# First rows scaled in place and transposed in a written order, one bank and the stores moved, and the first MLP product's weights copied ahead of the splits

## The chip, the cores and the metric

The kernel runs on one core of a Trainium2 chip. The metric is the device time of one execution in microseconds, as the median of several runs. Before the change it is 2446.93 us (three runs, 2443.65 to 2447.63).

## What is computed

One layer of a decoder trunk on a sequence of 512 rows of 2048 channels, all in float32. Cut to what matters:

```
h = rmsnorm(x, g_mix)
cb, cc, cv, q, k, v, f_logit, gate_c, gate_a = split(h @ w_in)
conv_branch = (cb * causal_dwconv(cc * cv, conv_w)) @ w_conv_out
attn_branch = forgetting_attention(q, k, v, log_sigmoid(f_logit + b_f)) @ w_attn_out
x = x + (sigmoid(gate_c + b) * conv_branch + sigmoid(gate_a + b) * attn_branch) @ w_mix_out
h = rmsnorm(x, g_mlp)
x = x + square(relu(h @ w_ff1)) @ w_ff2
out = rmsnorm(x, g_final)
```

Here rmsnorm(x, g) is x / sqrt(mean(x*x) + eps) * g, row by row. Nearly all the time goes to the large products: w_in (2048 x 10248), w_ff1 (2048 x 8192) and w_ff2 (8192 x 2048).

## The kernel before

**Products.** A product in float32 is made of three: each operand is split into a high part (ACT's copy to the rounded type fp32r, buffer th for weights) and a low part (DVE's difference between the operand and its high part, buffer tl). PE then adds high x high, high x low and low x high into a bank of PSUM (lines 149, 151, 153 with weights standing and rows moving; lines 167, 169, 172 the other way round). There are two buffers th and two tl.

**Groups.** The products with w_in and w_ff1 are made in groups of two by two blocks by a scheme that needs seven products in place of eight (A11, A12, S4, S3, S2, A22, S1; class Group). The rows' operands of the same names (A11, A12, A22 and the sums S1 to S4) are made once and held in tiles. A group has four accumulators a, b, c, d, and its argument `banks` says in which of the eight banks each lies. `begin` makes A11 (into a) and A12 (into b), `rest` the other five. A product is one step of a pipeline (class Pipe, line 188 on): in each step the sources of one product are split on ACT and DVE, the product split a step before is put on PE, and the one before that is evacuated from its bank (`snap`, ACT, line 294; `plus`, DVE, line 112). Other work hangs on the steps by `pipe.fill(n, work)`, which runs it n steps later. Within `with manual():` the order of the instructions on each engine is the order in which the program writes them; outside, the framework's scheduler orders them by priority and readiness.

**The opening (lines 554 to 627).** The rows x come in four blocks t of 128 rows (tile xn, line 562), each of 1 MB, all queued on SP ahead of the first weights (line 274). For each block ACT squares and sums the rows (line 496), DVE adds the sums up (line 491) and POOL takes the inverse root (line 492), which gives a factor r per row. DVE puts r on the diagonal of a 128 x 128 tile dg (line 526). PE multiplies 128 x 128 pieces of the rows with dg (line 530), four to a bank, banks 6 and 7 in turn: that transposes and scales at once. Each such float32 matmul appears twice in the trace, as two passes. DVE multiplies the bank with the gain per channel (tile cols) into h, in two instructions, one for even and one for odd pieces of channels (line 535). Then the halves of A11, A12 and A22 that this block of rows fills are split (lines 105 and 106). All of this is ordered by the scheduler, together with what follows: five groups of which only `begin` is made at first, gV0 (a part of the attention's V) and four key-and-query groups (`heads`), while the sums for S1 to S4 are made beside them. Among these groups b lies in bank 3 for all five.

**The MLP's start (lines 1530 to 1552).** The last rows of the second norm are turned and summed while the first group g0 of w_ff1 runs its A11 and A12, in a written order: `Q2.sums(3, behind)` makes the high parts of S1, S3, S2, S4 on ACT (line 1152) and the low parts of S4 and S3 on DVE, then `g0.rest` begins with S4, whose weights ACT copies to th (line 248). `behind` holds the low parts of S2 and S1.

**The MLP's groups.** There are 16. Each evacuated half j is squared into r and summed (`sums`), and one step later split into rh and r and stored by two transfers on POOL's queue (`store`, lines 1248 to 1252). r and rh have one buffer each. Accumulator a lies in bank 4 for the first group and in banks 4 and 2 in turn from the second on.

## Time and profile before

| | us |
|---|---|
| median of three runs | 2446.93 (2443.65 to 2447.63) |
| the profiled execution | 2438.63 |
| its span, first to last instruction | 2436.9 |
| PE busy | 2412.2 |
| DVE busy | 1969.9 |
| ACT busy | 1169.0 |
| POOL busy | 238.5 |

PE is the matmul engine and PEld its weight loads, which run beside it; DVE is the vector engine, ACT the scalar engine, POOL GpSimd, SP SyncE, which issues loads. L149 is line 149 of the kernel. A row of the timeline gives start and length in us, the engine, the line, the operation, what is written and read, the shape, a count, and in brackets the idle time ahead of it with what ended it. A row of waits gives who waited for whom, the total in us, how often, and the longest. A row of stretches gives the stretch, its length, then busy time and count of PE, PEld, DVE, ACT and POOL, the granted clock as a share of full, the share of DMA and GB/s. A row of groups gives the line, the operation, its tiles and shape, the count, busy time in us and mean ns of one, and the idle time ahead.

### The profile page before, as it was taken

To read this page: it belongs to the slowest core of one execution; us is meant where nothing else is said; L and a number is where in the kernel's file an instruction comes from. 1 tells how busy PE (TensorE), PEld (TensorE's weight loads), DVE (VectorE), ACT (ScalarE), POOL (GpSimd) and SP (SyncE) were. 2 spreads that over 40 slices of the span, in tenths; PEclk is the share of its full clock that TensorE was granted. 3 is DMA by queue.
4 is the path that set the end of the run, shared out by engine and by line. 5 is a ranking of instruction groups with operands and counts; after the bars stand their busy time and mean duration, and the time that the engine had idled before them with its cause. 6 is when DMAs were issued, how large, how long until landed. Compare 5 with 4: busy or idle time off the path is not lost. (4 is left out here: it accounts for less than half of the span.)

```text
span 2436.9 us, 39812 instructions
## 1 busy us (share of the span) xinstructions
PE 2412.2 (99%) x17199; PEld 2242.7 (92%) x17199; DVE 1969.9 (81%) x1633; ACT 1169.0 (48%) x1184; POOL 238.5 (10%) x383
## 2 busy tenths in 40 slices
PE   8999999999999999999999999999999999999998
PEld 8999999999999998888899999999998888888886
DVE  7877677768887786735789888988988888888888
ACT  6443444444445563235556666665655333333334
POOL 0100011111210210100000000000010001100000
PEclk9999999999999999999999999999999999999999
DMA  7654434445664655536555655656588577655662
GB/s 251 182 180 156 152 122 147 153 142 163 210 197 131 204 169 169 186 121 216 164 199 179 211 205 185 242 187 219 190 292 284 199 244 242 232 186 198 230 225 87
DMA packets 268707, 466.17 MB, mean 191 GB/s; under 512 B 10524, under 2 KB 176532, under 8 KB 268404
## 3 DMA queue, kind: packets, MB, share of 16 engines
q1 hardware_dynamic: 224768, 283.72, 36.9%
q0 software_dynamic: 42896, 178.28, 20.0%
q8 instruction: 135, 2.21, 0.4%
q10 hardware_dynamic: 868, 1.62, 0.2%
q14 instruction: 40, 0.33, 0.0%
HBM read 369.74 MB, written 93.85 MB: 190 GB/s over the span
## 5 line engine op out<-in xcount | busy, mean ns | idle before, releaser
L248 ACT ACTIVATE th<-x 128x2048 fp32r<-128x2048 f32 (+2 forms) x280 | 513.2, 1833 | 499.1 <-PE a L151 150.1
L109 DVE TENSOR_TENSOR tl<-x,th 128x2048 fp32r<-128x2048 f32 (+2 forms) x280 | 610.6, 2181 | 144.2 <-ACT th L248 142.9
L109 DVE TENSOR_TENSOR x<-x,x 128x2048 f32<-128x2048 f32 (+1 forms) x108 | 246.9, 2287 | 36.8 <-DMA x<-in_w_ff_dram 36.7
L248 ACT ACTIVATE th<-y 128x2048 fp32r<-128x2048 f32 x66 | 126.7, 1922 | 200.8 <-PE a L169 99.1
L149 PE MATMUL a<-ST,th 128*128 128x256 f32 x768 | 177.6, 277 | 0.9 <-ACT o L294 0.9
L151 PE MATMUL a<-ST,th 128*128 128x256 f32 x768 | 177.3, 277 | 0.0
L167 PE MATMUL a<-th,us 128*128 128x512 f32 x512 | 161.1, 392 | 1.7 <-ACT x L1382 0.8
L248 ACT ACTIVATE th<-t 128x2048 fp32r<-128x2048 f32 x46 | 88.2, 1918 | 152.8 <-PE a L169 87.2
L109 DVE TENSOR_TENSOR tl<-y,th 128x2048 fp32r<-128x2048 f32 x66 | 150.8, 2286 | 10.8 <-ACT th L248 10.6
L169 PE MATMUL a<-th,us 128*128 128x512 f32 x512 | 158.5, 389 | 0.0
L106 DVE TENSOR_TENSOR tl<-raw,th 128x2048 fp32r<-128x2048 f32 x32 | 73.4, 2292 | 94.9 <-ACT th L105 94.7
L149 PEld LDWEIGHTS a<-ST,th 128*128 128x128 f32 x768 | 144.3, 188 | 1.3 <-ACT o L294 1.3
L109 DVE TENSOR_TENSOR tl<-t,th 128x2048 fp32r<-128x2048 f32 x46 | 105.3, 2289 | 48.7 <-ACT th L248 48.7
L151 PEld LDWEIGHTS a<-ST,th 128*128 128x128 f32 x768 | 144.3, 188 | 0.0
L482 PE MATMUL pn<-th,m 128*128 128x512 f32 x512 | 134.4, 391 | 0.0
L149 PE MATMUL a<-S,th 128*128 128x256 f32 x576 | 133.8, 278 | 0.0
L151 PE MATMUL a<-S,th 128*128 128x256 f32 x576 | 132.8, 276 | 0.0
L172 PE MATMUL a<-tl,us 128*128 128x512 f32 x512 | 126.6, 389 | 0.0
L167 PEld LDWEIGHTS a<-th,us 128*128 128x128 f32 x512 | 96.0, 188 | 26.2 <-DVE x L1384 3.4
L149 PE MATMUL d<-ST,th 128*128 128x256 f32 x512 | 118.4, 277 | 0.0
L151 PE MATMUL d<-ST,th 128*128 128x256 f32 x512 | 118.3, 277 | 0.0
L172 PEld LDWEIGHTS a<-tl,us 128*128 128x128 f32 x512 | 96.1, 188 | 19.9
(341 smaller groups left out, 6236.7 us busy)
## 6 DMA issues: line engine op xcount, KB each, us to landing
x<-in_w_in_dram SPq DMA_DIRECT2D x86, 1024.0 KB, 5.8
x<-in_w_ff_dram SPq DMA_DIRECT2D x64, 1024.0 KB, 7.8
y<-in_w_ff_dram SPq DMA_DIRECT2D x64, 1024.0 KB, 7.0
us<-s_d POOLq DMA_DIRECT2D x42, 1024.0 KB, 8.9
s_d<-rh POOLq DMA_DIRECT2D x32, 896.0 KB, 6.6
s_d<-r POOLq DMA_DIRECT2D x32, 896.0 KB, 7.6
raw<-in_w_mix_out_dram SPq DMA_DIRECT2D x24, 1024.0 KB, 5.1
g_d<-o POOLq DMA_DIRECT2D x32, 256.0 KB, 2.6
```

The lines of the kernel that those rows point to most:

```text
L106: nc.vector.tensor_tensor(out=lo, in0=src, in1=hi.bitcast(F32), op=ALU.subtract)
L109: nc.vector.tensor_tensor(out=out, in0=a, in1=b, op=ALU.subtract)
L149: nc.tensor.matmul(o, hi[:, q, js], Sh, start=first and q == 0 and j == 0, stop=False, skip_group_check=True)
L151: nc.tensor.matmul(o, hi[:, q, js], Sl, start=False, stop=False, skip_group_check=True)
L167: nc.tensor.matmul(o, Sh[:, ts], hi[:, q, :], start=begin, stop=False, skip_group_check=True)
L169: nc.tensor.matmul(o, Sl[:, ts], hi[:, q, :], start=False, stop=False, skip_group_check=True)
L172: nc.tensor.matmul(o, Sh[:, ts], lo[:, q, :], start=False, stop=q == nq - 1, skip_group_check=True)
L248: nc.scalar.activation(out=self.hi, in_=self.src, func=AF.Copy)
L482: nc.tensor.matmul(ps[t], A[t][e], w[:, q, :], start=first, stop=last)
```

## The change

It has five parts.

1. *The opening.* `block` is replaced by `scaled` (the rows are multiplied with r in place, on DVE, in two or four pieces), `turn` (16 transposes with the identity into four banks at once) and `gained` (one instruction per bank, even and odd pieces together). H is renumbered so that both lie in one tile. Block 0 and block 1 are done in a written order (`rows_in`); blocks 2 and 3 are left to the scheduler.
2. *Loads.* The first two weight loads of gV0 are queued on SP between the rows of block 1 and those of block 2.
3. *Banks.* The second key-and-query group's b lies in bank 6. In the MLP, a alternates the other way: bank 2 for the second group, then 4, and so on; the last group's c changes with it.
4. *Stores.* In all MLP groups but the last two, the store of the second half comes one step later.
5. *The MLP's start.* The copy of S4's weights to th is made right behind A22's split, ahead of the four sums' high parts.

On PE, at the program's start; ptr is the bank into which rows are turned, dg the diagonal and ident the identity, th and A the weights and rows of the first products a and b. Before:

```order
L573 MATMUL pv<-ident,rows 128x88
L530 MATMUL ptr<-dg,xn 128x128 x36
L167 MATMUL a<-th,A_146 128x256
L530 MATMUL ptr<-dg,xn 128x128 x4
L167 MATMUL a<-th,A_146 128x256
L530 MATMUL ptr<-dg,xn 128x128 x4
L169 MATMUL a<-th,A_146 128x256 x2
```

And now, where the line numbers are those of the changed kernel:

```order
L590 MATMUL pv<-ident,rows 128x88
L535 MATMUL ptr<-ident,xn 128x128 x32
L167 MATMUL a<-th,A_142 128x256 x2
L169 MATMUL a<-th,A_142 128x256
L167 MATMUL b<-th,A_143 128x256 x2
L169 MATMUL a<-th,A_142 128x256
L167 MATMUL a<-th,A_142 128x256 x2
```

Before, block 2's pieces were turned ahead of and among the first matmuls of a; now blocks 0 and 1 come first, and blocks 2 and 3 follow in two runs of 16 within a's end and b. Two matmuls of b stand ahead of a's fourth.

On DVE, at the same place; v is the sum of squares, r the factor, h the rows turned and gained, A_142 and A_146 are A11, and x_147 the first weights. Before:

```order
L491 TENSOR_REDUCE v<-ss_144 128x1
L526 TENSOR_SCALAR dg<-ident,r 128x128
L642 CAST identb<-ident 128x128
L574 COPY cols<-pv 128x88
L491 TENSOR_REDUCE v<-ss_144 128x1
L535 TENSOR_TENSOR h_148<-ptr,cols 128x2x128
L535 TENSOR_TENSOR h_149<-ptr,cols 128x2x128
L526 TENSOR_SCALAR dg<-ident,r 128x128
```

And now:

```order
L491 TENSOR_REDUCE v<-ss_140 128x1
L529 TENSOR_SCALAR xn<-xn,r 128x512
L591 COPY cols<-pv 128x88
L529 TENSOR_SCALAR xn<-xn,r 128x512 x3
L549 TENSOR_TENSOR h_144<-ptr,cols 128x2x2x128 x2
L678 CAST identb<-ident 128x128
L549 TENSOR_TENSOR h_144<-ptr,cols 128x2x2x128
L491 TENSOR_REDUCE v<-ss_140 128x1
L529 TENSOR_SCALAR xn<-xn,r 128x1024 x2
L549 TENSOR_TENSOR h_144<-ptr,cols 128x2x2x128 x5
L106 TENSOR_TENSOR A_142<-h_144,A_142 128x8x128
L109 TENSOR_TENSOR tl<-x_147,th 128x2048
```

Block 1's reduction stood ahead of all gains; three gains of block 0 now stand ahead of it, and the first weights' low part stands between A11's two halves.

On ACT, at the start of the MLP; ST are the rows' operands (the first row is A22's high part, the L1152 and L1189 rows those of S1, S3, S2 and S4), x_12097 and x_12086 the weights of S4, and o the evacuated A11. Before:

```order
L105 ACTIVATE ST<-down 128x512
L1152 ACTIVATE ST<-down 128x512
L1152 ACTIVATE ST<-up 128x512 x2
L1152 ACTIVATE ST<-down 128x512
L248 ACTIVATE th<-x_12097 128x2048
L294 ACTIVATE o<-a 128x512
```

And now:

```order
L105 ACTIVATE ST<-down 128x512
L248 ACTIVATE th<-x_12086 128x2048
L1189 ACTIVATE ST<-down 128x512
L1189 ACTIVATE ST<-up 128x512 x2
L1189 ACTIVATE ST<-down 128x512
L294 ACTIVATE o<-a 128x512
```

The weights' copy has moved ahead of the four high parts; DVE's order is the same there. Beyond these places, only the stores of part 4 (on ACT and DVE) and the order of the sums beside the key-and-query groups differ.

The diff:

```diff
 
 
         def __init__(self, view, c1, c2, w, ST, mm, banks, put, scale=1.0, extra={}, nq=KT // 2, spot=None):
-            self.extra, self.nq, self.spot = extra, nq, spot
+            self.extra, self.nq, self.spot, self.s4 = extra, nq, spot, None
             self.view, self.cs, self.w, self.ST, self.mm, self.banks = view, (c1, c2), w, ST, mm, banks
             self.put, self.scale, self.at, self.X, self.A = put, scale, {}, {}, {}
 
...
                 self.put(1, 1, r["d1"])
                 self.put(0, 1, r["s4"])
 
-            pipe.step(self.product("S4", (1, 1), "c", True), after=next(turns), guest=True)
+            pipe.step(self.s4 or self.product("S4", (1, 1), "c", True), after=next(turns), guest=True)
             hook("S4")
             p = self.product("S3", (0, 1), "d", True)
             p.evict = s3
...
                 self.tiles(n)
             self.h1 = self.quad(pair(PLACE["S1"], F32, "h1"))
             self.h2 = self.quad(ph.tile([P, 2, D], F32, tag="h", name="h2"))
-            self.H = {(0, 0): self.h1[:, 1], (1, 0): self.h1[:, 0], (0, 1): self.h2[:, 1], (1, 1): self.h2[:, 0]}
+            self.H = {(i, par): h[:, par] for i, h in enumerate((self.h1, self.h2)) for par in range(2)}
 
         def moving(self, n):
             return moving(self.ST[n])
...
         def put(self, n, src, ts=slice(0, HS)):
             split(src[:, :, ts], self.ST[n][:, 0, :, ts], self.ST[n][:, 1, :, ts])
 
-        def block(self, xt, part, t):
+        def scaled(self, xt, part, e, n=2):
             r = rstd_of(part)
-            i, ts = t // 2, slice(t % 2 * P, (t % 2 + 1) * P)
-            dg = const.tile([P, P], F32, tag="dg", name="dg", bufs=2)
-            nc.vector.tensor_scalar(out=dg, in0=ident, scalar1=r, scalar2=None, op0=ALU.mult)
-            for c in range(4):
-                pt = bank(6 + c % 2, "ptr")
+            for c in range(n):
+                h = xt[:, c * D // n:(c + 1) * D // n]
+                if e == "A":
+                    nc.scalar.activation(out=h, in_=h, func=AF.Copy, scale=r)
+                else:
+                    nc.vector.tensor_scalar(out=h, in0=h, scalar1=r, scalar2=None, op0=ALU.mult)
+
+        def turn(self, xt, banks):
+            pts = [bank(b, "ptr") for b in banks]
+            for c, pt in enumerate(pts):
                 for k in range(4):
-                    nc.tensor.matmul(pt[:, k * P:(k + 1) * P], xt[:, (4 * c + k) * P:(4 * c + k + 1) * P], dg,
-                                     start=True, stop=True)
-                p2 = pt.rearrange("p (q two b) -> p two q b", two=2, b=P)
-                g2 = self.gT[:, 4 * c:4 * c + 4].rearrange("p (q two) -> p two q", two=2)
-                for par in range(2):
-                    nc.vector.tensor_tensor(out=self.H[i, par][:, 2 * c:2 * c + 2, ts], in0=p2[:, par],
-                                            in1=g2[:, par].unsqueeze(2).to_broadcast([P, 2, P]), op=ALU.mult)
-            if i == 0:
-                self.put("A11", self.H[0, 0], ts)
-                self.put("A12", self.H[0, 1], ts)
-            else:
-                self.put("A22", self.H[1, 1], ts)
+                    nc.tensor.transpose(pt[:, k * P:(k + 1) * P], xt[:, (4 * c + k) * P:(4 * c + k + 1) * P], ident)
+            return pts
+
+        def gained(self, t, pts, cs=range(4), act=False):
+            ts = slice(t % 2 * P, (t % 2 + 1) * P)
+            for c in cs:
+                o = (self.h1, self.h2)[t // 2][:, :, 2 * c:2 * c + 2, ts]
+                if act:
+                    for k in range(4):
+                        nc.scalar.activation(out=o[:, k % 2, k // 2], in_=pts[c][:, k * P:(k + 1) * P], func=AF.Copy,
+                                             scale=self.gT[:, 4 * c + k:4 * c + k + 1])
+                else:
+                    p2 = pts[c].rearrange("p (q two b) -> p two q b", two=2, b=P)
+                    g2 = self.gT[:, 4 * c:4 * c + 4].rearrange("p (q two) -> p two q", two=2)
+                    nc.vector.tensor_tensor(out=o, in0=p2, in1=g2.unsqueeze(3).to_broadcast([P, 2, 2, P]), op=ALU.mult)
+
+        def half(self, n, t):
+            i, par = {"A11": (0, 0), "A12": (0, 1), "A22": (1, 1)}[n]
+            if n not in self.ST:
+                self.tiles(n)
+            self.put(n, self.H[i, par], slice(t % 2 * P, (t % 2 + 1) * P))
 
         def sums(self):
             H = self.H
...
     px = ph.enter_context(phase("px"))
     xin = []
     xp = [pair(2 + i, F32, "xn") for i in range(2)]
-    for t in range(NT):
+    def load_x(t):
         h = xp[t // 2][:, t % 2]
         n = 4 if t == 0 else 2
         for i in range(n):
             nc.sync.dma_start(out=h[:, i * D // n:(i + 1) * D // n], in_=x[t * P:(t + 1) * P, i * D // n:(i + 1) * D // n])
         xin.append(h)
+
+    for t in range(2):
+        load_x(t)
         if t == 0:
             rows = main.tile([NV, P], F32, tag="x3", name="rows")
             r0 = 0
...
         for i in range(4):
             square_part(xin[t][:, i * S:(i + 1) * S], ss1[:, t, i:i + 1], junk[:, i * S:(i + 1) * S])
 
-    for t in (0, 1):
-        squares(t)
-        Q1.block(xin[t], ss1[:, t, :], t)
-    for t in (2, 3):
-        squares(t)
-    Q1.tiles("A22")
-    for t in (2, 3):
-        Q1.block(xin[t], ss1[:, t, :], t)
-
+    def first_loads():
+        for n in "0123":
+            if n in "01":
+                gV0.load(int(n), 0)
+            else:
+                load_x(int(n))
+
+    def rows_in():
+        squares(0)
+        Q1.scaled(xin[0], ss1[:, 0, :], "D", 4)
+        pts = Q1.turn(xin[0], (6, 7, 5, 2))
+        squares(1)
+        Q1.gained(0, pts, range(3))
+        Q1.scaled(xin[1], ss1[:, 1, :], "D")
+        Q1.gained(0, pts, (3,))
+        pts = Q1.turn(xin[1], (0, 1, 6, 7))
+        Q1.gained(1, pts)
+        for n, t in (("A11", 0), ("A11", 1), ("A12", 0), ("A12", 1)):
+            Q1.half(n, t)
 
     def store_v(c0, w):
         def put(i, j, v):
...
     def steady(n):
         return ((2 + n % 2,), (3 - n % 2,), (0,), (1,))
 
-    heads = [gV0] + [kq(hp, ((a,), (3,), (3 + hp % 2 * 3,), (7,))) for hp, a in enumerate((0, 1, 2, 5))]
+    heads = [gV0] + [kq(hp, ((a,), (6 if hp == 1 else 3,), (3 + hp % 2 * 3,), (7,))) for hp, a in enumerate((0, 1, 2, 5))]
+    first_loads()
+    with manual():
+        rows_in()
+    for t in (2, 3):
+        squares(t)
+    for t in (2, 3):
+        Q1.scaled(xin[t], ss1[:, t, :], "DD"[t - 2])
+        Q1.gained(t, Q1.turn(xin[t], (6, 7, 5, 2)))
+        Q1.half("A22", t)
     for g in heads:
         g.begin()
         g.order = ((1, 1), (0, 1), (0, 0), (1, 0))
...
             self.put("A11", c, self.F[0, c][0])
             self.put("A12", c, self.F[0, c][1])
 
-        def sums(self, c, rest=None):
+        def sums(self, c, rest=None, then=lambda: None):
             (a11, a12), (a21, a22) = self.F[0, c], self.F[1, c]
             self.put("A22", c, a22)
+            then()
             add(a22, a21, a22)
             sub(a21, a11, a21)
             sub(a11, a22, a11)
...
                 held.append(c)
             elif j == 0 or ((0, 1) in quarters and (1, 1) in quarters):
                 for n, work in zip(SUMS[j], (sums, store)):
-                    pipe.fill(n + (LATER[j][work is store] if g == DFF // S - 1 else 0), lambda work=work: work(j))
+                    pipe.fill(n + (LATER[j][work is store] if g == DFF // S - 1 else j * (work is store and g < DFF // S - 2)),
+                              lambda work=work: work(j))
 
         return put
 
...
     def banks1(g):
         if g == 0:
             return (4,), (0,), (1,), (7,)
-        return (2 + 2 * (g % 2),), (3,), (1 if g < DFF // S - 1 else 2,), (7 if g < DFF // S - 1 else 5,)
+        return (4 - 2 * (g % 2),), (3,), (1 if g < DFF // S - 1 else 4,), (7 if g < DFF // S - 1 else 5,)
 
     groups = [ff1(g, banks1(g)) for g in range(DFF // S)]
     US = ((4, ("A11", "A12")), (0, ("S2", "S3")), (1, ("S1", "A22")), (2, ("S4",)))
...
         squares_of_rows()
         Q2.gained(1, 3)
         behind = []
-        Q2.sums(3, behind)
+        g0.s4 = g0.product("S4", (1, 1), "c", True)
+        Q2.sums(3, behind, g0.s4.high)
         mean = []
 
         def at(n):
```

## The prediction, made before the changed kernel had run

> **What bounds the kernel now.** I read the page first, then the waits of the matmul engine, then a table of stretches, then the timeline at the places where it waits.
>
> ```profile
> span 2436.9 us, 39812 instructions
> PE 2412.2 (99%) x17199; PEld 2242.7 (92%) x17199; DVE 1969.9 (81%) x1633; ACT 1169.0 (48%) x1184; POOL 238.5 (10%) x383
> ```
>
> PE is busy 2412.2 of 2436.9 us. The change takes one pass away from each of 64 small matmuls and no work from any product, so it can win little beside the 24.7 us in which PE stands. The waits say where that is:
>
> ```profile
> PE pv L573 <- DMA rows<-in_conv_w_dram: 6.1, 1, 6.1
> ...
> PE a L149 <- ACT o L294: 0.9, 2, 0.7
> PE d L142 <- ACT th L248: 0.8, 1, 0.8
> ...
> PE a L153 <- DVE tl L109: 0.6, 1, 0.6
> PE b L149 <- DVE o L112: 0.4, 1, 0.4
> ```
>
> The table (PE, PEld, DVE, ACT and POOL busy with counts, granted clock, DMA share, GB/s) puts them at two places:
>
> ```profile
> 0.00:20.00 20.00, 9.34 (x57) 8.49 (x57) 8.08 (x27) 14.43 (x37) 2.80 (x12) 1.00 0.89 300
> 20.00:40.00 20.00, 19.53 (x168) 19.46 (x169) 17.44 (x29) 10.21 (x8) 0.55 (x1) 1.00 0.79 240
> 40.00:80.00 40.00, 39.59 (x349) 39.43 (x349) 39.11 (x24) 24.05 (x17) 6.39 (x8) 1.00 0.71 211
> 1195.00:1240.00 45.00, 42.73 (x368) 41.98 (x367) 36.38 (x32) 25.01 (x28) 2.32 (x3) 1.00 0.41 129
> 1240.00:1800.00 560.00, 559.79 (x4917) 559.53 (x4916) 492.02 (x365) 350.05 (x350) 32.62 (x60) 1.00 0.59 206
> ```
>
> The opening loses over 10 us, the start of the MLP 2.3, and the MLP's steady groups nothing. The last row gives the price of a 256-wide matmul, 560/4917 = 0.114 us, and of a product of 48, 5.47. DVE is full from 40 to 80 us, so there it is nearly a second bound.
>
> **The opening.** Every engine's later work is the same, so I ask when the first key-and-query product starts; before it starts at 40.05. These rows of the timeline carry the steps:
>
> ```profile
> 8.53 3.78 PE L530 MATMUL ptr<-dg,xn 128*128 128x128 f32 x16 [2.04 <-DMA bf<-in_b_f_dram]
> 13.11 5.18 PE L530 MATMUL ptr<-dg,xn 128*128 128x128 f32 x40 [0.80 <-PE ptr L530]
> 20.47 2.02 PE L530 MATMUL ptr<-dg,xn 128*128 128x128 f32 x16 [2.18 <-DVE h L535]
> 26.64 1.95 PE L530 MATMUL ptr<-dg,xn 128*128 128x128 f32 x16
> 40.05 0.29 PE L149 MATMUL a<-A,th 128*128 128x256 f32 x1
> 12.18 0.16 DVE L491 TENSOR_REDUCE v<-ss 128x1 f32<-128x5 f32 x1 [3.41 <-ACT junk L496]
> 13.01 0.29 DVE L526 TENSOR_SCALAR dg<-ident,r 128x128 f32<-128x128 f32 x1
> 17.64 2.35 DVE L106 TENSOR_TENSOR A<-h,A 128x1024 fp32r<-128x1024 f32 x2
> 2431.43 0.75 DVE L1502 TENSOR_SCALAR x<-x,r 128x1024 f32<-128x1024 f32 x1
> L535 DVE TENSOR_TENSOR h<-ptr,cols 128x256 f32<-128x256 f32 x32 | 11.8, 418 | 1.1 <-PE ptr L530 1.1
> 43.66 0.69 DVE L112 TENSOR_TENSOR o<-b,o 128x512 f32<-128x512 f32 x1
> 44.26 2.28 DVE L112 TENSOR_TENSOR h<-h,h 128x2048 f32<-128x2048 f32 x1
> 46.46 2.29 DVE L109 TENSOR_TENSOR tl<-x,th 128x2048 fp32r<-128x2048 f32 x1
> 19.41 1.89 ACT L248 ACTIVATE th<-x 128x2048 fp32r<-128x2048 f32 x1
> ```
>
> Before, 64 matmuls with the diagonal run as 128 passes. A pass takes 1.95/16 = 0.122 us. The 64 transposes with the identity I take at one such pass each: PE loses 64 x 0.122 = 7.8 us of work. DVE pays: ten scalings, four of 512 (about 0.41, between the 0.29 at 128 and the 0.75 at 1024) and six of 1024 (about 0.7), are 5.8 us, against four diagonals of 0.29. The 32 gains of 256 (11.8 us) become 16 of 512. One of these I take at 0.61, from the step 43.66 to 44.26 of an addition that also reads a bank; its bound above is two gains of 256, 0.74. DVE does 2.7 us more in all.
>
> DVE is also what sets the pace. Before, the reduction at 12.18 stood in DVE's order ahead of the first gains and held them 3.41 us. Now three gains of row block 0 run in that time. The squares of row block 1 still end at 12.2, since its loads keep their place, and its factor is ready at 13.0. Then, in DVE's written order: two scalings, 1.4, to 14.4; five gains, 3.05, to 17.45; A11's low half of block 0, 1.17, to 18.6; the low part of the first weights, 2.2 (the step 44.26 to 46.46 of as large an operation), to 20.8; A11's low half of block 1, to 22.0. Only there can PE run on; it has done five matmuls of the products by then. ACT has to keep up. The first product's two weight loads now go right behind block 1, whose last piece is on hand at 10.8:
>
> ```profile
> 10.81 0.63 ACT L496 ACTIVATE junk<-xn 128x512 f32<-128x512 f32 x1 [0.28 <-DMA xn<-in_x_dram]
> 10.00:20.00 10.00, 7.49 (x51) 6.83 (x50) 7.14 (x18) 9.38 (x25) 1.11 (x2) 1.00 1.05 377
> 16.29 1.99 ACT L105 ACTIVATE A<-h 128x1024 fp32r<-128x1024 f32 x2
> ```
>
> At 377 GB/s a load of 1024 KB takes 2.8 us: the two land near 13.6 and 16.4. From there ACT copies the second weights (1.89) and three halves (1.0 to 1.05 each), to 21.4, just ahead of DVE. At the 300 GB/s of the first 20 us it would be 22.7, 0.7 late, which is a bound. Blocks 2 and 3 are in by 22 to 25, ahead of their squares or a microsecond behind.
>
> From 22.0 PE has 91 matmuls, 10.4 us, and 32 transposes, 3.9, and waits some 0.4 for DVE's scaling of block 2 (ready near 27.4 and 28.1: 22.0 + 2.35 + 0.16 + 2.2 + 1.4). That gives 36.65, **3.4 us earlier** than 40.05.
>
> This is if PE runs at its full rate from 22.0. The first 16 passes after PE's long stand took 3.78 us, 0.236 each, and from 13.11 on the rate was full; so a start from rest costs half the rate for 3.8 to 4.6 us (8.53 to 13.11), though the granted clock reads 1.00 there. A stand of 2.18 us (before 20.47) did not bring it back. In the changed kernel PE stands from about 15.4 to 22.0 but for five matmuls. That is nearer to the first case, so I take a half rate for 4.2 us: 2.1 lost, of which 0.4 would have been waiting. **The opening then gains 1.7 us**, the first key-and-query product at 38.4.
>
> The Trainium skill, page TensorE: Matmul & The Clock Gate, Part 1: The HAM clock gate, says that the array falls to half its clock after an idle window of about 3.4 us and needs about as long busy to return. By that rule the half rate would last 3.4 us and the sum below would be 3.5 us in place of 3.1. The same page's Part 4: PE-mode transpose says that transposes do not count as activity that raises the clock; by that, block 1's transposes too would run at half rate, and the sum would be some 0.55 us smaller. No row here shows transposes alone.
>
> **A bank among the key-and-query groups.**
>
> ```profile
> 67.84 0.36 PE L149 MATMUL b<-A,th 128*128 128x256 f32 x1 [0.41 <-DVE o L112]
> ```
>
> The third group's b waited for the addition that empties bank 3. With the second group in bank 6 this wait of 0.41 goes. The next late is the fourth group, which needs bank 3 from the third. ACT copies the second key-and-query weights when the product before is through with its high parts, 16 matmuls ahead of 38.4, at 36.6; that copy, A22's last half and its low part bring DVE to 40.7. From there to the addition that empties bank 3 it has 15 operations of 2.2, four additions of 0.61 and 0.3 of pauses: 76.4. PE is there at 38.4 + 7 x 5.47 = 76.7. With so little to spare I count 0.2 (0 to 0.41).
>
> **The start of the MLP.**
>
> ```profile
> 1202.99 0.63 ACT L1152 ACTIVATE ST<-down 128x512 fp32r<-128x512 f32 x1 [1.48 <-DVE down L112]
> 1205.71 1.90 ACT L248 ACTIVATE th<-x 128x2048 fp32r<-128x2048 f32 x1
> 1207.64 2.29 DVE L109 TENSOR_TENSOR tl<-x,th 128x2048 fp32r<-128x2048 f32 x1 [0.52 <-ACT th L248]
> 1214.20 0.35 PE L142 MATMUL d<-ST,th 128*128 128x192 f32 x1 [0.81 <-ACT th L248]
> 1237.97 0.39 PE L149 MATMUL a<-ST,th 128*128 128x256 f32 x1 [0.69 <-ACT o L294]
> ```
>
> S4's high copy (1.90) moves into ACT's 1.48 us of waiting. The copy overruns by 0.3, but the split that DVE needs first, S4's at 1205.17, waits for DVE's own subtraction and is not late. DVE's 0.52 of waiting goes, its chain up to S3's weights comes 0.5 earlier, and PE's 0.81 shrinks to 0.3: **0.5 us** (0.2 to 0.81). What is next late is DVE itself, which still has PE waiting 0.6 at S2.
>
> The second group's first product took bank 4, from which the first group's last was still being read; it now takes bank 2. Its weights are long split, so **0.7 us** goes (0.6 to 0.85, with the refill).
>
> **The stores.** In the first 14 of 16 groups the copy to the second store's buffer moves behind the high copy of the next group's first weights, and the store comes some 2.7 us later. PE stood nowhere in these groups, so I count nothing. The next group reuses the buffer:
>
> ```profile
> 1386.91 0.53 POOL L1252 DMA_DIRECT2D s_d<-r  x1 [1.66 <-DVE r L1249]
> 1399.91 0.62 ACT L1234 ACTIVATE r<-c 128x512 f32<-128x512 f32 x1
> ```
>
> From 1386.9 + 2.7 and the 7.6 us median landing it is free at 1397.2, ahead of 1399.9. If that cover went, ACT's wait would push the next weights' copy, due at 1401.0, by as much; PE needs it several microseconds later, so two late microseconds still cost nothing.
>
> ```profile
> s_d<-r POOLq DMA_DIRECT2D x32, 896.0 KB, 7.6
> ```
>
> **Sum.** 1.7 + 0.2 + 0.5 + 0.7 = 3.1 us. The profiled execution took 2438.63 (span 2436.9 and 1.7 around it), so 2435.5 by it. That run is 5.0 below the lowest of the timed ones and 8.3 below their median, 2446.93, so I carry the difference to the median: **2443.8**. A measurement here can tell about 0.2%, 4.9 us, from no change; the timed runs themselves spread over 4.0.
>
> **Rivals.** *PE keeps its full rate* through the stand at 15 to 22 us, helped by the five matmuls in it: the opening gains 3.4, the sum is 4.8, 2442.1. For it: 2.18 us did no harm. Against: three times as long. Chance 0.30, the forecast's 0.50.
>
> *DVE becomes the bound in the opening and among the first groups.* It does 2.7 us more work, was full from 40 to 80, and the two bank handovers have no margin. With gains at 0.74, 16 x 0.13 = 2.1 us come on top and PE waits for them: sum 1.0, 2445.9. For it: the gains write with four strides. Against: the addition row reads a bank at 0.61. Chance 0.14.
>
> *PE's half rate lasts through both first products*, because the two blocks of transposes among them break its run again: 14.3 us of work take 28.6, the first key-and-query product starts at 50.6, 10.5 later than before; with 1.4 gained behind it that is 9.1 slower, 2456.0. To be slower by over 4.9 it must cost 9.7 us against the full rate. Against: before, one burst of 3.8 us and a short pause brought the full rate. Chance 0.06.
>
> That the edits do not do what they say is excluded by the order, but for the stores, which I count at nothing anyway.
>
> **Numbers.** The range, 2440.8 to 2446.8, reaches from all upper bounds at the full rate (3.4 + 0.41 + 0.81 + 0.85 = 5.5, 2441.4, and half a microsecond of spread) to the second rival with a microsecond more. Faster by over 0.2% is half of the first rival and a fifth of the forecast's case: 0.27 with some spread. Slower is the last rival and a little: 0.07. The rest, 0.66, is no change.
>
> **What would show it.** Right: one-pass transposes; PE's main run from about 22.0 with some 18 matmuls near 0.23 us each; the first key-and-query product at 38.4; no wait of b near 66; 0.3 in place of 0.81 and none of 0.69 at the MLP's start; matmuls at 0.114 us and no wait of PE in its groups. Wrong: matmuls at 0.114 from 22.0 on; gains of 0.74; a wait for weights or rows ahead of 22; new PE waits in the groups.

## The result, and the profile after

The changed kernel takes 2432.03 us (median of six runs, 2429.02 to 2435.09) beside 2447.28 for the kernel before in the same session (six runs, 2440.87 to 2451.46): 15 us less by the medians. The ratio estimated from all these runs is 0.9948 (95% interval 0.9931 to 0.9964), which is 12.7 us. The forecast was 2443.8 (2440.8 to 2446.8), and the measured time lies below that range. The new profiled execution took 2431.68, close to its median; the old one had taken 2438.63, quicker than every timed run of its kernel so far. So the two profiles show only 7 us of the gain. The page after:

```profile
span 2430.0 us, 39663 instructions
PE 2405.1 (99%) x17135; PEld 2237.5 (92%) x17135; DVE 1973.4 (81%) x1623; ACT 1172.1 (48%) x1184; POOL 239.8 (10%) x383
```

PE's waits after:

```profile
PE pv L590 <- DMA rows<-in_conv_w_dram: 6.1, 1, 6.1
PE ptr L535 <- DVE xn L529: 4.2, 2, 2.2
PE a L167 <- ACT A L105: 2.1, 1, 2.1
...
PE a L153 <- DVE tl L109: 0.6, 1, 0.6
...
PE d L142 <- ACT th L248: 0.3, 1, 0.3
```

The stretches after (columns as before):

```profile
20.00:40.00 20.00, 18.54 (x131) 17.68 (x131) 17.93 (x21) 12.49 (x24) 3.01 (x2) 0.83 0.71 230
40.00:80.00 40.00, 40.00 (x355) 40.00 (x354) 39.33 (x24) 23.79 (x16) 6.39 (x8) 1.00 0.73 214
1195.00:1240.00 45.00, 44.05 (x375) 43.53 (x374) 36.04 (x31) 24.84 (x28) 2.32 (x3) 1.00 0.42 130
1240.00:1800.00 560.00, 560.00 (x4939) 560.00 (x4938) 495.95 (x366) 354.17 (x352) 32.51 (x60) 1.00 0.59 208
```

The small steps went as forecast: no wait of b, 0.3 in place of 0.81 for S3's weights, no 0.69 at the second MLP group. New is the last row: PE was busy for 559.79 of the 560 us before as well, but made 4917 matmuls there and now 4939: 22 more are 2.5 us. A busy PE can still be a slower PE. The opening after, on the timeline of PE and of DVE, and DVE's groups between 5 and 45 us:

```profile
8.62 3.68 PE L535 MATMUL ptr<-ident,xn 128*128 128x128 f32 x16 [2.15 <-DVE xn L529]
14.31 3.56 PE L535 MATMUL ptr<-ident,xn 128*128 128x128 f32 x16 [2.01 <-DVE xn L529]
23.12 0.58 PE L169 MATMUL a<-th,A 128*128 128x256 f32 x1 [0.52 <-DVE A L106]
27.77 0.45 PE L167 MATMUL a<-th,A 128*128 128x256 f32 x2
30.52 1.91 PE L535 MATMUL ptr<-ident,xn 128*128 128x128 f32 x16
39.65 0.28 PE L149 MATMUL a<-A,th 128*128 128x256 f32 x1
```

```profile
12.67 0.16 DVE L491 TENSOR_REDUCE v<-ss 128x1 f32<-128x5 f32 x1 [0.49 <-ACT junk L496]
14.83 1.32 DVE L549 TENSOR_TENSOR h<-ptr,cols 128x512 f32<-128x512 f32 x2
16.31 0.69 DVE L549 TENSOR_TENSOR h<-ptr,cols 128x512 f32<-128x512 f32 x1 [0.16 <-PE ptr L535]
17.16 1.44 DVE L549 TENSOR_TENSOR h<-ptr,cols 128x512 f32<-128x512 f32 x2 [0.16 <-PE ptr L535]
18.51 1.22 DVE L106 TENSOR_TENSOR A<-h,A 128x1024 fp32r<-128x1024 f32 x1
31.16 2.48 DVE L549 TENSOR_TENSOR h<-ptr,cols 128x512 f32<-128x512 f32 x4 [1.63 <-PE ptr L535]
```

```profile
L549 DVE TENSOR_TENSOR h<-ptr,cols 128x512 f32<-128x512 f32 x16 | 10.4, 686 | 2.1 <-PE ptr L535 2.0
L529 DVE TENSOR_SCALAR xn<-xn,r 128x1024 f32<-128x1024 f32 x6 | 4.2, 749 | 1.1 <-POOL r L492 1.1
```

A transpose is one pass, 1.91/16 = 0.12 us at full rate and 0.22 to 0.23 for blocks 0 and 1. PE's main run begins at 23.12 (22.0 was forecast), at half rate up to 27.77 (4.65 us; 4.2 was forecast), which the granted clock of 0.83 in 20 to 40 us shows too, and the first key-and-query product starts at 39.65, 1.25 later than forecast. Nearly all of that is there at 23.12 already. The reduction of row block 1 came at 12.67 in place of 12.2, and block 1's five gains with their pauses fill 14.83 to 18.51, 3.68 us where 3.05 was taken, because PE hands them its transposes at half rate; in `after_pad64`, told of below, these transposes ran at full rate and the same five take 3.07. The gain itself was sized well: four on end take 2.48, 0.62 each (the mean of 686 ns counts overlaps twice).

### The profile page after: what moved, and what is told of

Read it like the earlier page. It is cut to its first block, busy times and chain, and to the rows that moved or that the text cites. A ratio compares the mean times of both kernels' runs of the same rounds, so it can differ in the third digit from the quotient of the medians.

```text
span 2430.0 us, 39663 instructions
## 1 busy us (share of the span) xinstructions
PE 2405.1 (99%) x17135; PEld 2237.5 (92%) x17135; DVE 1973.4 (81%) x1623; ACT 1172.1 (48%) x1184; POOL 239.8 (10%) x383
## 4 chain that ended last, share of the span: by engine, by line
PE 95%; DVE 2%; DMA 1%; issue 1%; ACT 0%; POOL 0%; DVEq 0%; POOLq 0%; SPq 0%; ACTq 0%
PE a L153 8%; PE a L149 8%; PE a L151 8%; PE pn L482 7%; PE d L149 5%; PE d L151 5%; PE d L153 5%; PE a L169 5%; PE a L167 5%; PE a L172 5%; PE pt L1063 4%; PE b L149 3%; PE b L151 3%; PE c L149 3%; PE d L169 3%; PE d L167 3%
## 5 line engine op out<-in xcount | busy, mean ns | idle before, releaser
L109 DVE TENSOR_TENSOR tl<-y,th 128x2048 fp32r<-128x2048 f32 x66 | 150.9, 2287 | 12.2 <-ACT th L248 12.1
L151 PE MATMUL d<-ST,th 128*128 128x256 f32 x512 | 117.8, 276 | 0.0
```

What stands on the lines that cost most here:

```text
L109: nc.vector.tensor_tensor(out=out, in0=a, in1=b, op=ALU.subtract)
L151: nc.tensor.matmul(o, hi[:, q, js], Sl, start=False, stop=False, skip_group_check=True)
```

## The experiments

**One part at a time.** Four kernels of one session. `open_only` is the changed kernel with parts 3 (MLP), 4 and 5 undone; the others are the kernel before with one edit:

```diff
 stores_only
-pipe.fill(n + (LATER[j][work is store] if g == DFF // S - 1 else 0), lambda work=work: work(j))
+pipe.fill(n + (LATER[j][work is store] if g == DFF // S - 1 else j * (work is store and g < DFF // S - 2)),
+          lambda work=work: work(j))
 mlpbank_only
-return (2 + 2 * (g % 2),), (3,), (1 if g < DFF // S - 1 else 2,), (7 if g < DFF // S - 1 else 5,)
+return (4 - 2 * (g % 2),), (3,), (1 if g < DFF // S - 1 else 4,), (7 if g < DFF // S - 1 else 5,)
 s4_only
-Q2.sums(3, behind)
+g0.s4 = g0.product("S4", (1, 1), "c", True)
+Q2.sums(3, behind, g0.s4.high)
```

> The kernel before with the new opening alone (rows scaled in place, written order, one bank among the key-and-query groups); MLP banks, stores and S4's copy as before. Theory (the stores): what the timed runs gained beyond the forecast came from the stores, which let the MLP's weight loads land in time; then this kernel gains only what the two profiles show in the opening, 0.4 to 1.5 us, some 2446, and its DVE still waits 30 us or more in all for loads of w_ff. Rival (the opening): the median of the timed runs holds more than the one profile, and the opening gives most of the 15; then 2434 to 2438.

> The kernel before with the second store of each MLP group moved behind the next group's first high copy and nothing else. Theory (the stores): DVE's waits for w_ff fall from 36.7 us to a few, PE has no product of 5.65 us in the steady groups, and 8 to 13 us of the 15 are there: 2434 to 2439. Rival (the opening, or the bank): no change within 2 us, although DVE's waits for w_ff fall.

> The kernel before with the banks of the MLP's groups swapped and nothing else. Theory (the stores): PE's wait of 0.69 at the second group goes, 0.7 us faster, 2446.5, with DVE's waits for w_ff as before, 30 us or more. Rival (the slow step): where PE comes out of a short wait it may run on in a step of 117.5 ns per matmul in place of 113.3, so that each short wait less can save several us; then 3 to 8 us faster and fewer products of 5.65 us in the first half of the MLP.

> The kernel before with S4's high copy ahead of the splits at the MLP's start and nothing else. All theories: 0.3 to 0.8 us faster or no difference that can be seen, 2446.5. More than 3 us would speak for the slow step that begins or ends by such shifts.

Measured: `open_only` 2435.72 beside 2442.54, ratio 0.9973 (0.9963 to 0.9982); `stores_only` 0.9978 (0.9967 to 0.9990); `mlpbank_only` 1.0004 (0.9990 to 1.0017); `s4_only` 1.0002 (0.9990 to 1.0014). Neither theory holds alone: the opening gives 0.27%, some 6.7 us, far more than the 0.4 between the two profiles, and the stores 0.22%, 5.4 us (3.6 by the medians). What is left for the other parts is below what the runs can tell.

**Parts taken out again.** `open_no_bank` is `open_only` with bank 3 kept; `bank_only` is the kernel before with the one edit `(6 if hp == 1 else 3,)`; `no_stores` is the changed kernel with the stores back.

> The kernel before with the new opening alone and without the bank: the second key-and-query group keeps bank 3, so the wait of b at 65 us (0.41, 0.67 with its refill) is back. Theory (a late opening): in four profiles with the old opening the first key-and-query product started at 40.1, 40.1, 42.0 and 43.3, in two with the new one at 39.3 and 39.7, so the new opening is worth some 2 us on average, more than the 0.4 of the two profiles that I had; 1.5 to 4 us faster, and the first key-and-query product again at 39 to 40. Theory (the slow step): b's wait is followed in some executions by nine products of 5.65 us in place of 5.44 up to the 192-wide matmul at 114 us. Rival: the opening gains as much as with the bank, 6.7 us.

> The kernel before with bank 6 for the second key-and-query group and nothing else. Theory (the slow step): the wait of b goes, and with it the products of 5.65 us between 67 and 114 us that came after it in two of four profiles with the old opening: 0.7 us always and 1.7 more in about half of the executions, so 1 to 2.4 us faster, and in the profile no product above 5.5 us between 60 and 105 us. Rival (the wait alone): 0.4 to 0.7 us.

> The changed kernel with the stores where they were before. Theory (the stores): DVE's waits for w_ff are back at 30 us or more, products of 5.65 us and short waits return in the MLP's groups, and it is 3 to 6 us slower than the changed kernel, so 9 to 12 faster than the kernel before. Rival: the stores do not matter with the other edits in, so 14 to 16 faster.

Measured: 0.9974 (0.9963 to 0.9985), 0.9999 (0.9984 to 1.0013) and 0.9963 (0.9951 to 0.9976). The bank is worth nothing that the runs tell, with the new opening or without (an interval of 3 to 4 us either way can't exclude the 0.4 to 2.4 that were expected); the opening without it, which I put at 1.5 to 4 us, gains 0.26%, 6.4 us. Putting the stores back takes the gain from 0.52% to 0.37%, 3.7 us of the 3 to 6 expected, though the two intervals overlap.

**Where the time lies.** PE's order is the same in all these kernels behind the opening, so their profiles can be laid side by side. Times in us: the start of the first key-and-query product; from there to attention's first matmul; the first half of the MLP (from the mean's matmul to the first with w_ff2); the rest up to the last row of matmuls; the number of products of about 5.65 us in the MLP's steady groups (from the second on); the step from the second product with w_ff2 to the third, from the low parts of the one to those of the other, so that a wait of the third is in it. The expectations call this step ff2's second product. The six kernels with "pad" or "dummy" are told of below. Each row is a single profile.

```
                    kq start  to attn  w_ff1   w_ff2   5.65s  2nd w_ff2
old opening
 before             40.05   238.04  606.40  613.67   10    6.92
 before_again       45.17   239.72  613.42  612.73   37    7.91
 mlpbank_only       42.02   239.72  605.45  614.08    6    9.26
 s4_only            43.31   239.72  611.09  615.27   20   10.17
 bank_only          41.88   237.37  607.05  615.09    6    9.71
 before_pad64       45.13     -     609.50  612.05   19    7.10
 stores_only        40.13   238.04  603.46  613.85    0    7.46
new opening
 open_only          39.26   237.39  607.83  611.11    2    5.76
 open_no_bank       39.48   237.41  607.58  611.44   15    6.48
 no_stores          39.75   240.14  607.55  611.18   26    5.44
 after              39.65   237.41  602.41  610.42    0    5.44
 after_again        39.71   237.41  602.40  612.83    0    6.08
 after_pad64        38.37     -     601.26  612.76    0    7.47
 after_pad128       39.77     -     602.39  611.12    0    6.07
 no_dummies         39.38   237.40  600.47  612.04    0    6.05
 one_dummy          38.33   240.14  600.57  613.12    0    6.20
 kq_dummy           38.15   240.46  600.59  611.62    0    5.48
```

Four differences stand out. The old opening ends at 40.05 to 45.17, on average 42.5; the new one at 38.15 to 39.77, 39.2. That is 3.3 us. The way to attention gives 0.6 on average (239.05 for the five old ones with bank 3, 238.47 for the eight new ones). The first half of the MLP takes 608.4 with the stores where they were (nine profiles) and 602.4 with them moved (the five that kept all extra matmuls), 6.0 less, a part of it from the MLP's start. The rest takes 613.8 with the old opening and 611.65 with the new one (without `after_pad64`), 2.2 less. Together 12.1, where the medians of two sessions differ by 15.3 and 11.7 and their ratios say 12.7 and 11.7.

**Both kernels again.**

> The changed kernel itself, beside the last one and the kernel before on one chip. All theories: 13 to 17 us faster than the kernel before; first key-and-query product at 38 to 40 us, the MLP's first half in 601 to 603 us, ff2's second product in 5.4 to 6.5 us with the load it waits for landing 10.8 to 10.9 us after its issue.

> The kernel before itself, for a second profile of it. Theory (its one profile was one of its quicker executions): first key-and-query product at 40 to 45 us, the MLP's first half in 605 to 611, ff2's second product at 7 to 10 us, the load it waits for landing 11.8 us or more after its issue; ratio 1.000 within 0.001.

Measured: 0.9952 (0.9937 to 0.9967) and 1.0002 (0.9989 to 1.0014). The changed kernel's gain, 11.7 us, is less than the 13 to 17 expected. The stage times came as expected to 0.2 us but for the kernel before's first half of the MLP, at 613.42 even longer. The opening of `before_again`, on PE, DVE and ACT:

```profile
16.08 7.43 PE L530 MATMUL ptr<-dg,xn 128*128 128x128 f32 x40 [3.64 <-issue]
45.17 0.29 PE L149 MATMUL a<-A,th 128*128 128x256 f32 x1
15.14 0.16 DVE L491 TENSOR_REDUCE v<-ss 128x1 f32<-128x5 f32 x1 [6.25 <-ACT junk L496]
13.77 0.63 ACT L496 ACTIVATE junk<-xn 128x512 f32<-128x512 f32 x1 [2.57 <-DMA xn<-in_x_dram]
```

The second half of row block 1 is squared at 13.77, once it has landed, where the profile shown before had 10.81. DVE's reduction waits 6.25 us for it, block 0's gains stand behind that reduction, and PE's next 40 passes, which by the program's order need the banks that these gains empty, start after 3.64 us of idling (0.80 in the profile shown before) and take 7.43 us in place of 5.18. At the end it is 5.1. It was late in this way in three of the seven old-opening profiles (12.78, 12.91, 13.77, against 10.51 to 10.89); in two of the other four PE's half rate lasted longer (granted clock 0.91 in 20 to 40 us, against 1.00). With the new opening the same half starts at 10.86 to 11.36 in all ten profiles, and block 0's gains no longer stand behind that reduction. Whether the new order of the loads keeps it early was not tested by itself.

**The product of 5.65 us.** Matmuls of 256 columns come every 113.3 ns, 5.44 us for 48, or every 117.8 ns, 5.65 us, for many products on end. The stretches, first of `before_again`, then of `after_again`:

```profile
1400.00:1500.00 100.00, 100.00 (x884) 100.00 (x884) 87.30 (x66) 61.93 (x62) 5.31 (x10) 1.00 0.53 188
1560.00:1620.00 60.00, 60.00 (x512) 60.00 (x511) 54.90 (x41) 36.09 (x38) 3.19 (x6) 1.00 0.52 181
```

```profile
1560.00:1620.00 60.00, 60.00 (x532) 60.00 (x531) 51.47 (x38) 37.06 (x37) 3.73 (x7) 1.00 0.68 241
```

512 against 532 matmuls in 60 us, no idle time, and the granted clock reads 1.00 in both. In `before_again` the slower step held from 1541 to 1764 us. It began some 15 us behind a wait of PE of 0.57, where a run of 16 matmuls took 1.99 in place of 1.81. Among the first groups it is plainer: in three of the six old profiles with b's wait of 0.4 all products behind it take 5.65, 257 matmuls from 75 to 105 us (`before_again`), against 267 in `bank_only`, where that wait is gone (first `before_again`, then `bank_only`):

```profile
75.00:105.00 30.00, 30.00 (x257) 30.00 (x256) 27.73 (x16) 12.60 (x8) 4.77 (x6) 1.00 0.61 182
```

```profile
75.00:105.00 30.00, 30.00 (x267) 30.00 (x266) 26.65 (x16) 11.54 (x9) 4.78 (x6) 1.00 0.63 188
```

That the wait brings it on is not shown. In the other three of the six the wait was there and the slower step did not last, and in four of the ten profiles with the new opening these products all take 5.65 (again 257 in 75 to 105 us) though PE waits nowhere between 40 and 110 us.

What ends it is often a matmul of 192 columns, of which the kernel has one in every third MLP group or so. Leaving these out from the second group on (`else {}` in `ff1`), keeping one, and adding one ahead of A12 of the first key-and-query group:

> The changed kernel without the extra 192-wide matmuls in the MLP's groups from the second on (they compute nothing that is used). Theory (the slow step lasts until a matmul of another width or a wait breaks it): the slow step entered at the wait at 1224 us, left before at the 192-wide matmul at 1254, now goes on for dozens of products of 5.65 us, at 0.21 each: in the profile a long row of them, 5 to 20 us slower than the changed kernel. Rival (it dies out by itself, or is of the power supply): eight matmuls less, about 1 us faster, and as few slow products as in the changed kernel.

> The changed kernel with the 192-wide matmul kept in the second MLP group and left out of all later ones. Theory (the slow step begins at the waits of the MLP's start and ends at a matmul of another width; with the stores moved no wait follows): no execution 20 us longer, as three of twelve were without any, and seven matmuls less, 0.8 us faster than the changed kernel: 15 to 17 us faster than the kernel before. Rival (it begins in the steady groups as well): some executions 5 to 20 us longer.

> The changed kernel with one 192-wide matmul ahead of the second product of the first key-and-query group (about 45 us), and with the extra matmuls of the MLP's groups from the third on left out. Theory (the slow step ends at a matmul of another width): where the products ran at 5.65 us from the opening on up to the 192-wide matmul at 110 to 116 us (three of eight profiles with the new opening), they now do so up to 45 us at most: in this profile no product above 5.6 us between 50 and 105, and on average 0.5 us less than the changed kernel besides the 0.8 of the matmuls left out: 1 to 1.5 us faster than the changed kernel. Rival (the step is set by something else that lasts): products of 5.65 us up to 110 us in spite of it, in some profiles.

`no_dummies`: nine executions took 2427.80 to 2431.80 and three 2450.86, 2451.58 and 2454.24; median 2429.62, ratio 0.9962 (0.9937 to 0.9986). The step of 22 us is 105 products of 0.21 more, about the whole first half of the MLP; the one profile is of a quick execution, so that this is what fills the three others is worked out, not seen. `one_dummy`: 0.9950 (0.9938 to 0.9962), none of its five executions above 2432.57, and no product of 5.65 in the MLP of its profile, as the theory had it, though it is 12 us faster than the kernel before and not 15 to 17. That none of five was slow is weak evidence, since at three in twelve this would come by chance one time in four; with the six of `kq_dummy`, which leaves out the same matmuls, it is one in 24. `kq_dummy`: 0.9945 (0.9930 to 0.9959), but here the theory missed: its matmul at 43.80 ended nothing, and 75 to 105 us again hold 257. Over all profiles such a matmul stood behind a whole product at this step 29 times and ended it 24 times. Both are as fast as the changed kernel within what the runs tell; none is clearly better.

**Why the stores matter.** DVE's group that turns the weights in the MLP's steady groups, `before_again`, then `after_again`, then the row of waits in `stores_only`:

```profile
L109 DVE TENSOR_TENSOR x<-x,x 128x2048 f32<-128x2048 f32 (+1 forms) x108 | 246.8, 2285 | 29.0 <-DMA x<-in_w_ff_dram 28.9
...
x<-in_w_ff_dram SPq DMA_DIRECT2D x64, 1024.0 KB, 7.8
```

```profile
L109 DVE TENSOR_TENSOR x<-x,x 128x2048 f32<-128x2048 f32 (+1 forms) x108 | 246.8, 2285 | 0.0
...
x<-in_w_ff_dram SPq DMA_DIRECT2D x64, 1024.0 KB, 6.5
```

```profile
DVE x L109 <- DMA x<-in_w_ff_dram: 0.3, 1, 0.3
```

With the stores where they were, the loads land in 7.8 us and DVE waits 28.9 to 45.2 us for them in the nine profiles; with them moved, it is 6.5 and 0.0 to 0.7. The moved store itself, s_d<-r, lands in 4.9 us in the eight profiles (between 1270 and 1780 us) in place of 6.4 to 7.9. That fits transfers which ran beside each other before and no longer do, but no run shows this alone. The products of 5.65 go with it: 2 to 37 in the steady groups against none in eight profiles.

This is where the 5 us lay hidden. Behind the MLP's first 48 us, matmuls at the slower step cost 1.1 to 8.6 us in the nine profiles, 4.0 on average, and pauses between matmuls 0.4 to 3.6, 1.8 on average, both against 113.3 ns from start to start; with the stores moved they cost 0.0 and at most 0.2.

**The start of w_ff2.** Its third product waits for a chain that begins with the load of y: in the profiles without pads, 0.8 to 2.5 us with the old opening and at most 0.4 with the new one. In three of the old six PE then fell to half rate for some 3 us (granted clock 0.77 to 0.78 over that product), and the product took 7.5 to 7.7 us in place of 6.0; these are the three above 9 in the table. In the same profiles the load takes 11.7 to 12.3 us from its issue to DVE's use with the old opening and 10.7 to 10.8 with the new one. Between these two points, 4 to 7 us behind the issue, lies with the old one a load of instructions (taken to be PE's, since these loads move with the number of its matmuls). With the new one there is none, or one within 0.2 us of the issue, when little else is moving. I moved that by extra matmuls of 64 columns in front of S3 of the last key-and-query group:

```diff
+if extra == "pad" and part == 0 and q == 0:
+    for _ in range(64):
+        nc.tensor.matmul(ps[:, 0, :64], hi[:, q, :P], Sh[:, :64], start=True, stop=False, skip_group_check=True)
```

> The changed kernel with 64 extra 64-wide matmuls (unused, overwritten) at one place of the last key-and-query group, so that PE has as many instructions ahead of the MLP's second product as before. They cost about 4 us there. Theory (instruction loads): in five profiles with the old opening the second product of ff2 took 6.92 to 10.17 us, in five with the new one 5.44 to 6.48, because a load of PE's instructions fell 0 to 4 us behind ff2's start there, among full DMA engines, and fell elsewhere once 64 matmuls were gone; here it falls back, and that product takes 7 to 10 us again, the load of y that it waits for landing 11.5 us or more after its issue in place of 10.8. Rival (the earlier opening itself, or chance): 5.4 to 6.5 as in the changed kernel.

> The same with 128 such matmuls, some 8 us there. 128 matmuls are 256 instructions on PE, a whole block of the instruction load (2.21 MB in 135 packets), so the loads fall where they do in the changed kernel. Theory (instruction loads): ff2's second product takes 5.4 to 6.5, as in the changed kernel. Rival (more instructions or a later time is what hurts): 7 to 10, as with 64 or worse.

> The kernel before with the same 64 extra matmuls, some 4 us there: PE's instructions ahead of ff2 are now a whole block more than in the changed kernel. Theory (instruction loads): ff2's second product takes 5.4 to 6.5 in place of 7 to 10, so that the 64 useless matmuls cost next to nothing in all: within 2 us of the kernel before. Rival (chance, or the opening): 7 to 10, and 4 us slower than the kernel before.

They cost far more than I had said, 9.3 us for 64, and the 26 matmuls behind them ran at half rate (granted clock 0.50 from 208.9 to 214.2 us), so the totals (1.0008, 1.0054 and 1.0047) tell nothing here; the place does. `after_pad64` on the timeline:

```profile
199.38 9.32 PE L143 MATMUL d<-S,th 128*128 128x64 f32 x64
1828.29 2.29 DVE L109 TENSOR_TENSOR t<-y,y 128x2048 f32<-128x2048 f32 x1 [2.46 <-DMA y<-in_w_ff_dram]
```

Its DMA queues from y's issue on, 10.8 us (packets, MB and share; then KB each and us to landing):

```profile
q8 instruction: 1, 0.02, 0.5%
us<-s_d POOLq DMA_DIRECT2D x4, 1024.0 KB, 15.0
y<-in_w_ff_dram SPq DMA_DIRECT2D x1, 1024.0 KB, 11.6
```

And `after_pad128`, the same two views:

```profile
1840.65 2.29 DVE L109 TENSOR_TENSOR t<-y,y 128x2048 f32<-128x2048 f32 x1 [1.48 <-DMA y<-in_w_ff_dram]
```

```profile
us<-s_d POOLq DMA_DIRECT2D x4, 1024.0 KB, 13.8
y<-in_w_ff_dram SPq DMA_DIRECT2D x1, 1024.0 KB, 10.6
```

With 64 the instruction load is back in the window, y and the four loads of us in it land 1.0 and 1.2 later, and the step from the second product to the third takes 7.47; with 128 it is out of it again and the step takes 6.07. `before_pad64` missed: its instruction load moved out of the window too, 0.7 us ahead of y's issue, but the load of y still took 12.0 and the step 7.10. There the transfers queued ahead of it were still under way (0.69 MB moved in the 2 us behind the issue, 0.10 in `after_pad128`), which may be why. So the instruction load is shown as one cause, not as the only one.

## Why the prediction was wrong

- *The base.* "so I carry the difference to the median" is one of the two steps that failed; the other is the nothing put down for the stores. A profiled execution 8.3 below the median lacks something that the others have, and what it lacks can be just what the edits take away. The second profile of the same kernel is 12.9 longer, and that lies where the edits work: 5.1 in the opening, 1.7 on the way to attention, 7.0 in the first half of the MLP. Two profiles of the changed kernel differ by 1.2. Of the 12.1 us that the averages show, the two profiles first compared show 7, so some 5 were out of sight.
- *The opening* was put at 1.7 us, to a start at 38.4. Ten profiles give 39.2, 0.8 later, for block 1's transposes at half rate and its later squares; but against the 42.5 of seven profiles with the old opening that is 3.3. The half rate was forecast well, 4.2 us against 4.65. The Trainium skill (TensorE: Matmul & The Clock Gate, Part 4: PE-mode transpose) says that transposes do not raise the clock. The trace after agrees, with 3.56 us for block 1's 16, half rate behind block 0's, and so do six others of the ten; but in `after_pad64` and `kq_dummy` the same 16 took 1.97, the full rate, and in `one_dummy` 2.38. Those three are the ones that start the first key-and-query product at 38.15 to 38.37, close to the forecast. The window of about 3.4 us that the Trainium skill gives on the same page (Part 1: The HAM clock gate) is shorter than the 4.65 measured.
- *The bank* was put at 0.2. With the new opening, bank 3 made no wait either (`open_no_bank`).
- *The MLP's start* came as forecast: from A12's low parts to S3's it took 12.05 us in place of 12.65 (12.04 in `s4_only`), and the bank's wait is gone. In both profiles of the changed kernel five products at the slower step follow, 1.1 us that no term had.
- *The stores*: "PE stood nowhere in these groups, so I count nothing" was wrong. The wait of DVE for w_ff, 36.7 us in 13 waits of the profile before, was not weighed, and PE's loss hid in the rate of its matmuls. `stores_only` gained 5.4 us; the table's first half of the MLP says 5.0 (603.46 against 608.4).
- *The start of w_ff2* was in no term. It gave 2.2 us; the one cause shown is the instruction load, which moved because 64 matmuls left the program.
- The rivals: PE did not keep its full rate, DVE did not become the bound, and the half rate did not last. The outcome was none of these, and a gain this large was in none of them.

## What to carry to other kernels

Where a profiled execution lies off the median of the timed runs, take a second profile before costing an edit: the difference belongs to some stage. Compare stages by the count of matmuls per microsecond, not by idle time alone, since a fully busy PE lost 4% for 200 us on end here. And a wait of another engine that PE's slack seems to hide may be worth removing: DVE's waits for the weights cost PE nothing in most groups, and 5 us in all, mostly through matmuls that kept coming at the slower step.

## What the runs showed of the hardware

Three things were not expected. PE's matmuls of 256 columns settle at 113.3 or at 117.8 ns apart, at a granted clock of 1.00, and stay there, the slower for up to 37 products of one profile's steady groups. A matmul of 192 columns ended it 24 times of 29. In `before_again` it began some 15 us behind a wait of PE; `open_no_bank` has 15 products at it in the steady groups without any wait of PE there. What brings it on, and what inside PE makes the two, is open. Next, 64 matmuls of 64 columns on end, with no wait of PE, took the granted clock to 0.76 in their stretch (199.4 to 208.5 us in `after_pad64`) and 0.50 in the 5.3 us behind it. And instructions come as loads of 16 KB (2.20 MB in 134 packets) through the same DMA engines: where one of them fell into a full window, the loads of y and us beside it landed 1.0 to 1.2 us later, so that taking matmuls out in the opening changed a wait 1800 us further on.
